# Copies and scalings recorded for ScalarE and VectorE alike, in a two-layer transformer trunk

## The chip, the core and the metric

The kernel runs on one core of a Trainium2 chip. The names of the engines are those of the profile: PE is TensorE, the matrix engine, and PEld its weight loads; DVE is VectorE and ACT is ScalarE, the two elementwise engines; POOL is GpSimd; SP issues the DMAs. The metric is device time in microseconds. Three runs of the kernel before took 2407.23, 2414.03 and 2417.83 us, so the median is 2414.03 us.

## The reference

The input is one sequence of 2048 latent tokens and 256 context tokens, 1024 wide, in float32. Two layers follow each other. In each, a conditioning vector gives shift, scale and gate; the tokens are normalized, shifted and scaled, multiplied by one input projection, mixed by two branches, multiplied by one output projection, gated and added to the stream:

```python
mod_l = jax.nn.silu(c) @ ada_w[i] + ada_b[i]
hl = rms_norm(x, norm_g[i]) * (1.0 + sc_l[:, None]) + sh_l[:, None]
# even layer: chunked gated linear attention (4 heads) || RG-LRU (512 channels), both directions
# odd layer: windowed attention (8 query heads, window 128, context keys, sink) || retention (4 heads)
y = concat([branch_a * silu(gate_a), branch_b * silu(gate_b)])
x = x + g_l[:, None] * (y @ w_out)
```

A last RMS norm gives the output. Everything is float32.

## The kernel before

**Precision and tiling.** The large products are kept near float32 by splitting each operand in two. A high part is a copy rounded to fp32r, a low part is the rest: `h = copy(raw)`, `l = raw - h`. Three products, `wh*yh`, `wl*yh` and `wh*yl`, are added in PSUM. So each weight block of 128x512 costs one copy (ACT, `wh`, L1085) and one subtraction (DVE, `wl`, L1086), 496 times in all, and so does each activation: the normalized tokens (`ya`, L1372 and L1373), the branch outputs before the output projection (L1846/L1847, L1862/L1863), the attention probabilities (`ur`, L2137/L2138). The sequence is cut into one context piece of 256 tokens and four latent pieces of 512. The projections run in `fm_block` (weights stationary, L1211) and `tm_tiles` (tokens stationary, L1189), and their results leave PSUM through copies and scalings on ACT or DVE.

**The norm.** For each 128 tokens, `scale_x` squares and sums on ACT (L1316), takes the root on POOL (L1299) and multiplies by it on DVE (`xt`, L1318). PE transposes eight 128x128 blocks (L1363) into two PSUM banks. Each block leaves PSUM with a scale and a shift per partition into a tile `tm`: in layer 0 all four of a bank on DVE (L1370), in layer 1 the second and fourth on ACT (L1368). The split follows.

**What sets the order.** The kernel is not written out instruction by instruction. All calls go to a `Recorder`, and `Plan.add` stores each with its engine, its dependencies (byte ranges of tiles) and a cost in ns. `Plan.order` then plays a list schedule: at each step it takes the engine that can start first, and on it the ready operation with the highest rank, the length of the costliest path behind it. Slots of the rings (`wr`, `wh`, `wl`, `tm`, `tmp`, PSUM banks) are given out in this play as well, where they come free. `Plan.emit` writes the calls in the order of the planned starts. Each engine works through its own queue in this order, and semaphores hold an instruction until what it reads is there. A cost marked `PORT` is for work of DVE on SBUF alone, which in the plan does not overlap with POOL's work.

Which engine a copy or a scaling has is fixed by the line that records it: `S.copy`, `S.activation` for ACT, `V.tensor_copy`, `V.tensor_scalar` for DVE. Where two engines read one PSUM bank, they wait for each other on the chip (the trace shows it below), but the plan knows only of byte ranges there, and of the order of PE's writes to one buffer.

Of the kernel before, what the change touches and what calls it, by code (L numbers as in the profile page):

```python
# [120 lines left out]
class Buffer:  # L121
    def __init__(self, ring, seq, at):
        self.ring, self.seq, self.at = ring, seq, at
        self.spans = Spans(ring.cols * 4)
        self.users = []
        self.slot = self.tile = self.last = None


class Plan:
# [5 lines left out]
    def __init__(self, nc, scratch):  # L135
        self.nc = nc
        self.ops = []
        self.tiles = {}
        self.cells = {}
        self.space = scratch.tile([128, self.WIDE], F32, name="space")  # L140
        self.space_name = self.space.tensor.name
        self.used = 0
        self.starts, self.bufs = [], []
        self.open = None


# [20 lines left out]
    def add(self, eng, fn, args, kw, after=(), line=None):  # L167
        op = len(self.ops)
        deps = {}
        out = kw["out"] if "out" in kw else (args[0] if args and isinstance(args[0], bass.AP) else None)  # L170
        outs = [x for x in (out, kw.get("accum_out")) if x is not None]
        ins = [x for x in (*args, *kw.values()) if isinstance(x, bass.AP) and not any(x is y for y in outs)]
        takes = []
        for x in ins:
            self.touch(x, op, eng, False, deps, takes)
        for x in outs:
            self.touch(x, op, eng, True, deps, takes)
        deps.pop(op, None)
        for o in after:
            if not deps.get(o):  # L180
                deps[o] = False
        self.ops.append((eng, fn, args, kw, line, deps, self.cost(eng, fn.__name__, out, ins, kw), takes))
        return op

    def touch(self, ap, op, eng, write, deps, takes):
# [28 lines left out]
        if b:  # L214
# [93 lines left out]
    def wait(self, j, e):  # L308
# [7 lines left out]
        return lat + LAT[e]  # L316

    def links(self):
        n = len(self.ops)
        succ = [[] for _ in range(n)]  # L320
        for i, o in enumerate(self.ops):
            for j, data in o[5].items():
                d = 0.0 if data is None else self.wait(j, o[0])
                if data is not None and self.ops[j][0] == o[0] and not data:
                    d = 0.0
                succ[j].append((i, d))
        return succ
# [31 lines left out]
    def order(self, key):  # L359
# [3 lines left out]
        left = [len(o[5]) for o in ops]  # L363
        at, start, landed = [0.0] * n, [0.0] * n, [0.0] * n
        self.landed = landed
# [21 lines left out]
        def wake(r):  # L387
            for k in parked[r]:
                heapq.heappush(later[ops[k][0]], (at[k], k))
            parked[r] = []  # L390
# [31 lines left out]

        def place(i, t):

            got = []
            for b in ops[i][7]:
# [3 lines left out]
                for s, us in r.free:  # L430
                    if all(done[u] for u in us) and all(s is not x[1] for x in got):
                        x = 0.0
                        for u in us:
                            d = self.wait(u, ops[i][0])
                            x = max(x, landed[u] + LAT[ops[i][0]] if d is None else start[u] + d)
                        can.append((x, len(can), s, us))
# [8 lines left out]
        for i in range(n):  # L445
            if not left[i]:
                heapq.heappush(later[ops[i][0]], (0.0, i))
        count = 0
        while count < n:
            best = None  # L450
            for e in range(5):
                if now[e]:
                    t = free[e]
# [9 lines left out]
            while later[e] and later[e][0][0] <= t:  # L463
                i = heapq.heappop(later[e])[1]
                heapq.heappush(now[e], (key[i], i))
            i = heapq.heappop(now[e])[1]
            if e == PE and last in (SMALL, QUAD) and ops[i][6][2] != last:
                same = min((x for x in now[e] if ops[x[1]][6][2] == last), default=None)
                if same:
# [3 lines left out]
                    i = same[1]  # L473
            if ops[i][6][2] == PORT and port > t:
                free[e] = t
                heapq.heappush(later[e], (port, i))
                continue
            if ops[i][7]:
                got, other = place(i, t)
                if got is None:  # L480
# [3 lines left out]
                    else:  # L484
                        parked[other].append(i)
                    continue
                for b, s, us in got:
# [3 lines left out]
                    wake(b.ring)  # L491
            occ, lat, kind = ops[i][6]
            if kind == PORT:
                port = t + occ
            elif e == PE and kind != last:
# [6 lines left out]
                elif last == TR:  # L502
                    t -= min(82.0, max(0.0, t - at[i]))
                last = kind
# [9 lines left out]
            for b in uses.get(i, ()):  # L514
                b.left -= 1
                if not b.left:
                    r = b.ring
                    hand(r.gone.pop(id(b.slot), r), b.slot, b.users)
            for k, d in succ[i]:
                at[k] = max(at[k], landed[i] + LAT[ops[k][0]] if d is None else t + d)  # L520
                left[k] -= 1
                if not left[k]:
                    heapq.heappush(later[ops[k][0]], (at[k], k))
        return start, max(free)
# [2145 lines left out]
```

## Time and profile before

| | |
|---|---|
| median of three runs | 2414.03 us |
| profiled execution, whole | 2415.39 us |
| its span, first to last instruction | 2413.6 us |
| PE busy | 2179.4 us, 90% |
| DVE busy | 1844.9 us, 76% |
| ACT busy | 1272.6 us, 53% |
| POOL busy | 277.6 us, 12% |
| mean granted clock of PE | 0.950 |

PE is the busiest engine, and it idles for 234.2 us of the span. The granted clock is a share of 2.4 GHz, and its lower level, 0.5, is 1.2 GHz. Time at the lower level counts as busy while the matrix engine does half the work. The 2415.39 us of the profiled execution are 1.4 us above the median of the runs and 1.8 us above its own span.

### The profile page before, as it was taken

To read this page: it belongs to the slowest core of one execution; us is meant where nothing else is said; L and a number is where in the kernel's file an instruction comes from. 1 tells how busy PE (TensorE), PEld (TensorE's weight loads), DVE (VectorE), ACT (ScalarE), POOL (GpSimd) and SP (SyncE) were. 2 spreads that over 40 slices of the span, in tenths; PEclk is the share of its full clock that TensorE was granted. 3 is DMA by queue.
4 is the path that set the end of the run, shared out by engine and by line. 5 is a ranking of instruction groups with operands and counts; after the bars stand their busy time and mean duration, and the time that the engine had idled before them with its cause. 6 is when DMAs were issued, how large, how long until landed. Compare 5 with 4: busy or idle time off the path is not lost. (4 is left out here: it accounts for less than half of the span.)

```text
span 2413.6 us, 43459 instructions
## 1 busy us (share of the span) xinstructions
PE 2179.4 (90%) x15721; PEld 1955.4 (81%) x15721; DVE 1844.9 (76%) x3908; ACT 1272.6 (53%) x2721; POOL 277.6 (12%) x350
## 2 busy tenths in 40 slices
PE   6999979879988989788997999979998899899998
PEld 2978768768667978687896889978898798899897
DVE  3667887897899688568776788778887768888786
ACT  2364774655566576354345444465445534566553
POOL 1000110010011000102201122001211000201021
PEclk8999989989989989798998999989999999999999
DMA  8245435544534435764444454425454233526873
GB/s 238 60 115 146 139 91 143 144 144 111 160 109 145 115 86 170 231 187 132 140 121 127 122 150 149 150 76 151 126 162 135 76 89 117 158 79 202 272 242 134
DMA packets 372616, 340.49 MB, mean 141 GB/s; under 512 B 41832, under 2 KB 318768, under 8 KB 372400
## 3 DMA queue, kind: packets, MB, share of 16 engines
q1 hardware_dynamic: 372400, 337.71, 46.8%
q8 instruction: 123, 2.02, 0.3%
q14 instruction: 93, 0.76, 0.1%
HBM read 256.31 MB, written 67.67 MB: 134 GB/s over the span
## 5 line engine op out<-in xcount | busy, mean ns | idle before, releaser
L1211 PE MATMUL psum<-wh,ya 128*128 128x256 f32 x4416 | 858.3, 290 | 13.7 <-ACT wh L1085 4.1
L1211 PEld LDWEIGHTS psum<-wh,ya 128*128 128x128 f32 x4416 | 695.4, 193 | 27.5 <-DVE ya L1373 5.1
L1189 PE MATMUL psum<-ya,wh 128*128 128x256 f32 (+2 forms) x2864 | 687.7, 325 | 23.1 <-DVE tmp L1695 9.3
L1211 PE MATMUL psum<-wl,ya 128*128 128x256 f32 x2208 | 573.6, 289 | 10.7 <-DVE wl L1086 10.7
L1189 PEld LDWEIGHTS psum<-ya,wh 128*128 128x128 f32 (+1 forms) x2864 | 484.2, 192 | 65.8 <-DVE tmp L1695 10.1
L1085 ACT CAST wh<-wr 128x512 fp32r<-128x512 f32 x496 | 303.4, 619 | 358.9 <-PE psum L1189 153.2
L1086 DVE TENSOR_TENSOR wl<-wr,wh 128x512 fp32r<-128x512 f32 x496 | 352.1, 716 | 146.9 <-ACT wh L1085 132.2
L1189 PE MATMUL psum<-ya,wl 128*128 128x256 f32 (+2 forms) x1432 | 450.5, 325 | 5.7 <-DVE wl L1086 4.3
L1211 PEld LDWEIGHTS psum<-wl,ya 128*128 128x128 f32 x2208 | 399.2, 193 | 17.2 <-DVE wl L1086 13.4
L1189 PEld LDWEIGHTS psum<-ya,wl 128*128 128x128 f32 (+1 forms) x1432 | 270.8, 192 | 27.3 <-DVE wl L1086 5.8
L2110 ACT ACTIVATE ub<-ub,s_mx 128x640 f32<-128x640 f32 (+1 forms) x128 | 104.9, 820 | 79.4 <-DVE s_mx L2101 78.4
L2137 ACT CAST ur<-psum 128x512 fp32r<-128x512 f32 (+1 forms) x184 | 93.7, 522 | 93.7 <-PE psum L2135 82.3
L2135 PE MATMUL psum<-c_k_ident,ub 128*128 128x128 f32 x624 | 126.3, 286 | 10.8 <-ACT tm L1368 5.8
L2101 DVE CUSTOM_DVE_ANT_0 ub<-psum,uc 128x640 f32<-128x640 f32 (+2 forms) x128 | 108.4, 847 | 33.5 <-PE psum L2096 30.7
L2138 DVE TENSOR_TENSOR ur<-psum,ur 128x512 fp32r<-128x512 f32 (+1 forms) x184 | 109.3, 605 | 30.7 <-ACT ur L2137 27.9
L2052 DVE TENSOR_TENSOR tmp<-tmp,ub 32x512 f32<-32x512 f32 x144 | 113.2, 786 | 12.4 <-ACT tmp L2328 6.2
L1370 DVE TENSOR_SCALAR tm<-psum,aT,shT 128x128 f32<-128x128 f32 x216 | 78.0, 407 | 38.1 <-PE psum L1363 21.0
L2135 PEld LDWEIGHTS psum<-c_k_ident,ub 128*128 128x128 f32 x624 | 79.0, 145 | 22.7 <-ACT tm L1368 9.3
L2049 POOL TENSOR_TENSOR tmp<-tmp,ub 128x512 f32<-128x512 f32 x20 | 29.7, 1483 | 389.2 <-ACT tmp L2394 217.1
L1299 POOL TENSOR_TENSOR s_rstd<-s_rstd,mhalf 128x1 f32<-128x1 f32 (+2 forms) x88 | 71.1, 810 | 6.8
L1622 ACT ACTIVATE ub<-psum,gb 128x512 f32<-128x512 f32 (+3 forms) x96 | 51.7, 584 | 32.0 <-PE psum L1621 31.7
L2114 DVE TENSOR_SCALAR ub<-ub,s_rs 128x640 f32<-128x640 f32 (+1 forms) x128 | 65.3, 549 | 1.1
(318 smaller groups left out, 3635.9 us busy)
## 6 DMA issues: line engine op xcount, KB each, us to landing
wr<-in_o_w_in_dram SPq DMA_DIRECT2D x192, 256.0 KB, 3.0
wr<-in_e_w_in_dram SPq DMA_DIRECT2D x160, 256.0 KB, 3.1
wr<-in_e_w_out_dram SPq DMA_DIRECT2D x80, 256.0 KB, 3.2
tmp<-gl SPq DMA_DIRECT2D x64, 256.0 KB, 4.1
wr<-in_o_w_out_dram SPq DMA_DIRECT2D x64, 256.0 KB, 3.4
x1l<-tmp SPq DMA_DIRECT2D x40, 256.0 KB, 3.0
xt<-x1l SPq DMA_DIRECT2D x20, 512.0 KB, 4.2
ua<-in_ada_w_dram SPq DMA_DIRECT2D x32, 256.0 KB, 4.3
```

Source lines behind the costliest of these rows:

```text
L1085: S.copy(h[:, 0:n], raw[:, 0:n])
L1086: eng.tensor_tensor(l[:, 0:n], raw[:, 0:n], h.bitcast(F32)[:, 0:n], op=ALU.subtract)
L1189: T.matmul(ps[0:m, q * w:q * w + w], lhsT=a, rhs=b, start=(q == 0 and k == 0 and i == 0), stop=(q == n // w - 1 and k == 7 and i == 2))
L1211: T.matmul(ps, lhsT=a, rhs=b, start=(ti % 2 == 0 and k == 0 and i == 0), stop=((ti % 2 == 1 or ti == len(tiles) - 1) and k == 7 and i == 2))
L1299: G.tensor_tensor(r, r, mhalf[:, 0:n], op=ALU.pow)
L1370: V.tensor_scalar(tm[:, kk], src, sc, sh, op0=ALU.mult, op1=ALU.add)
L2052: V.tensor_tensor(rot.v[to], raw.v[fr], sinb.v[fr], op=ALU.mult)
L2101: V.tensor_tensor_reduce(out=P_[:, c0:c0 + cn], in0=sc[:, so + c0:so + c0 + cn], in1=mask[:, m0:m0 + cn], scale=1.0, scalar=m, op0=ALU.add ...
L2110: tab_act(EXP, out=Ps[h], in_=Ps[h], func=AF.Exp, scale=-1.0, bias=mx[:, h:h + 1], accum_out=sm[:, h:h + 1])
L2135: T.transpose(tr[:, i * 256 + h * 128:i * 256 + h * 128 + 128], Ps[h][:, kb * 128:kb * 128 + 128], ident)
L2137: S.copy(ph[:, 0:n], tr[:, 0:n])
L2138: V.tensor_tensor(pl[:, 0:n], tr[:, 0:n], ph.bitcast(F32)[:, 0:n], op=ALU.subtract)
```

## The change

`Plan.add` asks a new function, `other_form`, whether a recorded operation can be written for the other elementwise engine as well. It can be for plain copies (`scalar.copy` and `vector.tensor_copy`), for a multiplication with an optional addition (`tensor_scalar` and `activation` with `Copy` or `Identity`), if the output has at least 64 columns, nothing is BF16 and the shapes are equal. Such an operation stands in the ready lists of both engines, with a cost for each, and in `order` the engine that takes it first keeps it. The form used is then the one emitted. Waits are worked out for the engine that did take it (`after`). The second part is in `touch`: for a PSUM buffer, an operation now also depends on the last use of the same bank by each other engine, reads included. Costs, rank rule, rings and recorded operations are the same; the ranks still go by the engine at which an operation was recorded.

```diff
+        form = self.other_form(eng, fn.__name__, args, kw)
+        if form:
+            e, fn, args, kw = form
+            self.others[op] = (e, fn, args, kw, line, deps, self.cost(e, fn.__name__, out, ins, kw), takes)
...
+    def other_form(self, eng, name, args, kw):
...
+        if name in ("copy", "tensor_copy") and not kw:
+            out, x = args
+            form = self.copies[ACT + DVE - eng], (out, x), {}
+        elif name == "tensor_scalar" and kw.get("op0") == ALU.mult and kw.get("op1", ALU.add) == ALU.add:
...
+        if n < 64 or BF16 in (out.dtype, x.dtype) or out.shape != x.shape:
+            return None
+        return (ACT + DVE - eng, *form)
...
+            if b.ring.psum:
+                hi = max(y for _, y in runs(f0, free)) - 1
+                for k in range(f0 // 512, hi // 512 + 1):
+                    used = b.banks.setdefault(k, {})
+                    for e, o in used.items():
+                        if e != eng and o != op:
+                            deps.setdefault(o, False)
+                    used[eng] = op
...
         for i in range(n):
             if not left[i]:
-                heapq.heappush(later[ops[i][0]], (0.0, i))
+                for e in at[i]:
+                    heapq.heappush(later[e], (0.0, i))
...
+            op = ops[i] if ops[i][0] == e else self.others[i]
...
-            for k, d in succ[i]:
-                at[k] = max(at[k], landed[i] + LAT[ops[k][0]] if d is None else t + d)
+            for k, data in needs[i]:
                 left[k] -= 1
-                if not left[k]:
-                    heapq.heappush(later[ops[k][0]], (at[k], k))
+                for f in at[k]:
+                    d = self.after(i, f, data)
+                    at[k][f] = max(at[k][f], landed[i] + LAT[f] if d is None else t + d)
+                    if not left[k]:
+                        heapq.heappush(later[f], (at[k][f], k))
```

65 lines are added ahead of the model code, so a line of the kernel body is 65 higher in the changed kernel (L1370 is L1435 there).

Counted in the two programs, 314 operations leave DVE for ACT and 387 leave ACT for DVE; DVE has 3983 instructions where it had 3910, and ACT 2286 where it had 2359. Matmuls, DMAs, POOL's work and the 80 table loads of ACT keep their number. The large movers are:

| line | what it is | from ACT to DVE | from DVE to ACT |
|---|---|---|---|
| L1085 | high part of a weight block, SBUF | 89 of 496 | |
| L1846 | high part of a branch output, scaled, from PSUM | 39 of 68 | |
| L2137 | high part of probabilities, from PSUM | 36 of 184 | |
| L1368 | scale and shift in the norm, from PSUM | 35 of 72 | |
| L1372 | high part of the normalized tokens, SBUF | 27 of 72 | |
| L1370 | scale and shift in the norm, from PSUM | | 113 of 216 |
| L2114 | division of the probabilities, SBUF | | 60 of 128 |
| L1318 | tokens times their root, 128x1024, SBUF | | 24 of 36 |
| others | copies and scalings on some 37 more lines | 161 | 117 |

Of the 72 groups of four scalings that empty one bank in the norm, 36 alternate between DVE and ACT before; 25 are shared by the two in the changed kernel.

**Place A**, the norm of the second latent piece in layer 0 (near 310 to 320 us in the trace of before). On DVE before, the scalings of one bank (`tm_3099`) stand among the constants of layer 1 (`smc`, `s_la`, `tmp`), the shifts (`shT`) and the LRU block (`ur`, `lru_cf`, `ub`):

```order
L1017 TENSOR_TENSOR smc_2998<-smc_2998,smc_398 128x12
L1255 TENSOR_SCALAR shT<-psum,adab 128x2
L1019 SCALAR_TENSOR_TENSOR s_la_3097<-smc_2998,smc_2994 128x12
L1370 TENSOR_SCALAR tm_3099<-psum,aT,shT 128x128 x2
L1610 TENSOR_TENSOR ur<-ub,ur 128x256
L1370 TENSOR_SCALAR tm_3099<-psum,aT,shT 128x128 x2
L1655 COPY lru_cf<-ub 128x1
L1993 TENSOR_TENSOR tmp_3109<-tmp_3109,tmp_2970 128x128
L1675 TENSOR_TENSOR ub<-ub 128x510
```

On ACT in the changed kernel, near the same place (`tm_3022` and `tm_3055` are the two tiles of the piece's first 128 tokens):

```order
L1711 ACTIVATE ub<-ub,s_119 128x510 x2
L1749 ACTIVATE tmp_3016<-psum 128x512
L1435 ACTIVATE tm_3022<-psum,shT,aT 128x128 x4
L1548 COPY ub<-uc 64x4x64 x2
L1437 CAST ya<-tm_3022 128x4x128
L1435 ACTIVATE tm_3055<-psum,shT,aT 128x128 x4
L1147 CAST wh_3066<-wr_2955 128x4x32
L1437 CAST ya<-tm_3055 128x4x128
```

All eight scalings of these tokens now stand on ACT, each bank's four in a row; before, all eight were on DVE.

**Place B**, just ahead of it: the high parts of the next weight blocks. On ACT before (`wh_3034` and `wh_3038` are read by the next matmuls of a projection):

```order
L1684 ACTIVATE tmp_3031<-psum 128x512
L1483 COPY ub<-uc 64x4x64
L1085 CAST wh_3034<-wr_2868 128x512
L1085 CAST wh_3038<-wr_2879 128x512
L1082 CAST wh_3044<-wr_2956 128x4x32 x3
L1372 CAST ya<-tm_3018 128x4x128
L1609 CAST ur<-ub 128x256
```

On DVE in the changed kernel (`wh_2973` and `wh_2978` are the high parts of the same two blocks):

```order
L1150 CAST wh_2943<-wr_2728 128x512
L1151 TENSOR_TENSOR wl_2947<-wr_2728,wh_2943 128x512
L1706 TENSOR_TENSOR ub<-ub 128x510 x2
L1150 CAST wh_2973<-wr_2856 128x512
L1150 CAST wh_2978<-wr_2873 128x512
L1311 COPY uc<-psum 128x256
L1074 TENSOR_SCALAR smc_2992<-smc_398 128x12
```

Three copies of weight blocks now stand in DVE's queue, ahead of the constants (`smc`) and of the scan behind them.

**Place C**, the subtraction that ends the split of the tokens in place A. On DVE before:

```order
L1653 SCALAR_TENSOR_TENSOR ub<-ub,lru_cf 128x510
L1015 TENSOR_TENSOR smc_2998<-smc_2998,smc_2994 128x12
L1594 SCALAR_TENSOR_TENSOR ub<-ua_137,cw,ub 128x256
L1016 TENSOR_SCALAR smc_2998<-smc_2998 128x12
L1373 TENSOR_TENSOR ya<-tm_3018,ya 128x4x128
```

On DVE in the changed kernel (`ub<-ub,s_dec` is the state recurrence of the linear attention; L1438 is L1373 before):

```order
L1600 TENSOR_TENSOR uc<-ub 64x2x64
L1082 TENSOR_TENSOR smc_2996<-smc_2996,smc_398 128x12
L1577 SCALAR_TENSOR_TENSOR ub<-ub,s_dec_3011,psum 64x128
L1084 SCALAR_TENSOR_TENSOR s_la_3118<-smc_2996,smc_2992 128x12
L1583 SCALAR_TENSOR_TENSOR ub<-ub,s_dec_3011 64x128
L1438 TENSOR_TENSOR ya<-tm_3022,ya 128x4x128
```

Between the constants' first instruction (L1009) and this subtraction DVE has 37 rows before and 48 in the changed kernel: the scalings are gone from there, and steps of the linear attention have come in front.

## Rows read from the trace of the kernel before

**Rows 1.** Head and first part of the page; the list of cores.

```profile
span 2413.6 us, 43459 instructions
PE 2179.4 (90%) x15721; PEld 1955.4 (81%) x15721; DVE 1844.9 (76%) x3908; ACT 1272.6 (53%) x2721; POOL 277.6 (12%) x350
...
core 0: 2413.6 us, clock 0.950
```

**Rows 2.** Windows of 800 us: busy us and count by engine, clock, DMA, GB/s.

```profile
0.00:800.00 800.00, 703.33 (x4826) 583.58 (x4827) 610.64 (x1355) 454.88 (x795) 69.50 (x112) 0.94 0.47 134
1600.00:2400.00 800.00, 759.48 (x5723) 712.64 (x5722) 631.67 (x1356) 419.02 (x1067) 103.59 (x116) 0.99 0.47 147
```

**Rows 3.** Windows of 10 us, the same columns.

```profile
60.00:70.00 10.00, 9.31 (x77) 8.91 (x77) 9.81 (x26) 3.00 (x6) 0.00 (x0) 1.00 0.17 54
310.00:320.00 10.00, 3.37 (x14) 2.42 (x14) 9.97 (x36) 2.97 (x9) 0.00 (x0) 0.71 0.34 111
320.00:330.00 10.00, 7.43 (x45) 6.28 (x45) 9.87 (x34) 6.94 (x22) 0.75 (x2) 0.60 0.23 62
490.00:500.00 10.00, 3.14 (x24) 2.03 (x23) 10.00 (x22) 6.43 (x12) 2.52 (x4) 0.76 0.56 170
980.00:990.00 10.00, 5.48 (x20) 4.16 (x21) 5.74 (x15) 3.64 (x12) 0.42 (x1) 0.50 1.06 367
1020.00:1030.00 10.00, 10.00 (x86) 10.00 (x86) 4.99 (x8) 2.50 (x4) 0.00 (x0) 1.00 0.68 221
2320.00:2330.00 10.00, 10.00 (x87) 10.00 (x85) 9.41 (x21) 3.95 (x9) 1.14 (x3) 1.00 0.79 240
```

**Rows 4.** Waits of PE on two-form work: us, times, longest.

```profile
PE psum L1363 <- DVE xt L1318: 22.7, 7, 5.9
PE psum L1211 <- DVE wl L1086: 10.7, 7, 7.3
...
PE psum L1620 <- DVE ur L1610: 0.2, 1, 0.2
```

**Rows 5.** Waits of PE on the rest, first and last.

```profile
PE psum L2095 <- DVE s_mx L2101: 13.8, 16, 5.0
...
PE psum L1211 <- ACT junk L1832: 0.2, 1, 0.2
```

**Rows 6.** Waits of DVE and of ACT on each other.

```profile
DVE wl L1086 <- ACT wh L1085: 132.2, 102, 6.1
ACT tm L1368 <- DVE tm L1370: 51.1, 40, 5.0
```

**Rows 7.** Groups on DVE by form: busy us, mean ns of one, idle before.

```profile
L1086 DVE TENSOR_TENSOR wl<-wr,wh 128x512 fp32r<-128x512 f32 x496 | 352.1, 716 | 146.9 <-ACT wh L1085 132.2 <-PE psum L1189 7.6 <-issue 2.0
L1370 DVE TENSOR_SCALAR tm<-psum,aT,shT 128x128 f32<-128x128 f32 x216 | 78.0, 407 | 38.1 <-PE psum L1363 21.0 <-ACT tm L1368 16.7
L2114 DVE TENSOR_SCALAR ub<-ub,s_rs 128x640 f32<-128x640 f32 x112 | 58.2, 558 | 0.9
L1318 DVE TENSOR_SCALAR xt<-xt,s_rstd 128x1024 f32<-128x1024 f32 x32 | 24.8, 774 | 8.5 <-POOL s_rstd L1299 7.4 <-ACT tm L1368 0.9
L1785 DVE COPY ua<-psum 128x512 f32<-128x512 f32 x16 | 11.0, 687 | 6.0 <-PE psum L1189 5.9
L1552 DVE COPY uc<-ub 64x128 f32<-64x128 f32 x20 | 4.4, 218 | 0.5
```

**Rows 8.** Groups on ACT by form, the same columns.

```profile
L1085 ACT CAST wh<-wr 128x512 fp32r<-128x512 f32 x496 | 303.4, 619 | 358.9 <-PE psum L1189 153.2 <-PE psum L1211 128.7 <-DMA wr<-in_e_w_in_dram 25.6
L2110 ACT ACTIVATE ub<-ub,s_mx 128x640 f32<-128x640 f32 x112 | 93.3, 833 | 70.6 <-DVE s_mx L2101 69.7
L1316 ACT ACTIVATE tm<-xt 128x1024 bf16<-128x1024 f32 x32 | 33.8, 1056 | 7.9 <-DMA xt<-in_ctx_dram 4.5 <-DVE ya L1373 1.8 <-DMA xt<-x1l 1.7
L1368 ACT ACTIVATE tm<-psum,shT,aT 128x128 f32<-128x128 f32 x72 | 31.3, 458 | 51.1 <-DVE tm L1370 51.1
L2338 ACT COPY ub<-psum 128x512 f32<-128x512 f32 x16 | 9.4, 589 | 7.4 <-PE psum L1211 7.3
```

More of the change, by code (lines that the diff above doesn't have):

```diff
@@ L144, in __init__ @@
         self.open = None
+        self.others = {}
+        self.copies = {ACT: nc.scalar.copy, DVE: nc.vector.tensor_copy}
+        self.act, self.scale = nc.scalar.activation, nc.vector.tensor_scalar
     def buffer(self, ring):
@@ L182, in add @@
         self.ops.append((eng, fn, args, kw, line, deps, self.cost(eng, fn.__name__, out, ins, kw), takes))
-        return op
+        form = self.other_form(eng, fn.__name__, args, kw)
+        if form:
+            e, fn, args, kw = form
+            self.others[op] = (e, fn, args, kw, line, deps, self.cost(e, fn.__name__, out, ins, kw), takes)
+        return op
+    def other_form(self, eng, name, args, kw):
+        if eng not in (DVE, ACT):
+            return None
[3 more added lines that the diff above has]
+        elif name == "tensor_scalar" and kw.get("op0") == ALU.mult and kw.get("op1", ALU.add) == ALU.add:
+            out, x, a, b = args
+            if b is None:
+                form = self.act, (), dict(out=out, in_=x, func=AF.Copy, scale=a)
+            elif isinstance(a, float) or isinstance(b, float):
+                return None
+            else:
+                form = self.act, (), dict(out=out, in_=x, func=AF.Identity, scale=a, bias=b)
+        elif name == "activation" and kw["func"] == AF.Identity and set(kw) == {"out", "in_", "func", "scale", "bias"}:
+            out, x = kw["out"], kw["in_"]
+            form = self.scale, (out, x, kw["scale"], kw["bias"]), dict(op0=ALU.mult, op1=ALU.add)
+        elif name == "activation" and kw["func"] == AF.Copy and set(kw) == {"out", "in_", "func", "scale"}:
+            out, x = kw["out"], kw["in_"]
+            form = self.scale, (out, x, kw["scale"], None), dict(op0=ALU.mult)
+        else:
+            return None
+        n = 1
+        for k in out.shape[1:]:
+            n *= k
+        if n < 64 or BF16 in (out.dtype, x.dtype) or out.shape != x.shape:
+            return None
+        return (ACT + DVE - eng, *form)
     def touch(self, ap, op, eng, write, deps, takes):
@@ L316, in wait, with after @@
         return lat + LAT[e]
+    def after(self, j, e, data):
+        if data is None:
+            return 0.0
+        return 0.0 if self.ops[j][0] == e and not data else self.wait(j, e)
     def links(self):
@@ L322, in links @@
             for j, data in o[5].items():
[L323 to L326, printed above, removed]
+                succ[j].append((i, self.after(j, o[0], data)))
         return succ
@@ L363, in order @@
         left = [len(o[5]) for o in ops]
-        at, start, landed = [0.0] * n, [0.0] * n, [0.0] * n
+        start, landed = [0.0] * n, [0.0] * n
+        at = [{o[0]: 0.0} for o in ops]
+        for i, o in self.others.items():
+            at[i][o[0]] = 0.0
+        needs = [[] for _ in range(n)]
+        for i, o in enumerate(ops):
+            for j, data in o[5].items():
+                needs[j].append((i, data))
         self.landed = landed
@@ L387, in wake @@
         def wake(r):
-            for k in parked[r]:
-                heapq.heappush(later[ops[k][0]], (at[k], k))
+            for k, e in parked[r]:
+                heapq.heappush(later[e], (at[k][e], k))
             parked[r] = []
@@ L451, in order @@
             for e in range(5):
+                for q in (now[e], later[e]):
+                    while q and done[q[0][1]]:
+                        heapq.heappop(q)
                 if now[e]:
@@ L464, in order @@
                 i = heapq.heappop(later[e])[1]
-                heapq.heappush(now[e], (key[i], i))
+                if not done[i]:
+                    heapq.heappush(now[e], (key[i], i))
             i = heapq.heappop(now[e])[1]
@@ L478, in order @@
             if ops[i][7]:
-                got, other = place(i, t)
+                got, other = place(i, e, t)
                 if got is None:
```

17 lines of the change are left out of this document (9 added, 8 removed).

## The prediction

> **What bounds the kernel now.** I read the head of the page first: PE is busy for 2179.4 of 2413.6 us, so it idles for 234.2 us, and its mean clock is 0.950 [rows 1]. The idle time has to be found before any edit can be priced. The windows of 800 us say where it is not: from 1600 us on PE is busy for 759.5 of 800 us at a clock of 0.99, while in the first third it has 703.3 at 0.94 [rows 2]. What can be won lies before 1600 us.
>
> Windows of 10 us say what the other engines did meanwhile [rows 3]. From 310 to 330 us PE was busy for 3.37 and 7.43 us and DVE for 9.97 and 9.87, with ACT at 2.97 and 6.94. From 490 to 500 DVE had 10.00, ACT 6.43, PE 3.14. Of the 240 such windows up to 2400 us, 62 show DVE at 9.3 or more (the first at 60 us, the last at 2320). They hold 78 us of PE's idle time, and 48 of them, with ACT under 7.5, hold 64 us. So about a quarter of the idle time falls where DVE's queue is full and ACT has room. The rest lies where neither is full (980 us: DVE 5.74, ACT 3.64, PE 5.48): chains of dependent steps and loads.
>
> Then the waits of PE by releaser. I put them into two heaps. In the first, the releaser is an operation that the change can move or the subtraction right behind one: 33 rows with 104 waits, 118.0 us together, from the tokens' scaling L1318 with 22.7 us down to 0.2 us [rows 4]. In the second it is something else (scores, state steps, DMAs): 22 rows, 77 waits, 98.5 us, from 13.8 us down [rows 5]. The two make 216.5 of the 234.2 us.
>
> Idle time costs twice. At 980 us the clock stood at 0.50, the 1.2 GHz level, and 20 matmuls ran in 10 us; at 1020 us, at the 2.4 GHz level, 86 did [rows 3]. A mean clock of 0.950 is 0.05 x 2413.6 = 121 us of full-clock work not done [rows 1], against 234 us of idle time: 0.52 us for each us of idle. I price idle time that goes or comes at 1.52.
>
> **The work that moves.** Leaving DVE are 314 operations. L1370: 113 x 407 ns = 46.0 us on DVE, and at the 458 ns of the same step on ACT 51.8 us there. L1318: 24 x 774 ns = 18.6 us; on ACT the square of the same tile takes 1056 ns without a pointer operand, and a pointer adds about 105 ns (833 ns for 640 columns with one, against 619 + 128 x 0.85 = 728 without, the 0.85 ns a column from 619 and 1056), so 24 x 1161 = 27.9 us. L2114: 60 at about 550 = 33 us on DVE, 60 at about 825 = 49 us on ACT. The other 117 lie between 218 ns (64x128) and 687 ns each: 26 to 80 us, taken as 44 by their shapes, and 47 on ACT. Sum: 142 us off DVE, 176 us onto ACT [rows 7, 8].
>
> Leaving ACT are 387. The largest, 89 copies of a 128x512 block from SBUF (619 ns on ACT, 55.1 us), have no like on DVE in the trace. The bounds are 218 ns (a copy a quarter as long) and 716 ns (two sources, same size). The single-source scalings cost 558 ns for 640 columns and 774 for 1024, that is 0.5625 ns a column; 218 + 384 x 0.5625 = 434 ns is what I take, since those rows also read SBUF alone: 38.6 us, with 19.4 and 63.7 us as the ends. The Trainium skill, "VectorE: DVE Perf Modes", section "The perf-mode tier table", gives float32 copies between SBUF tiles twice the rate of operations with two tensors; an estimate from its cycles, (150 + 256) / 0.96 = 423 ns, would make the 89 copies 37.6 us. No run here shows it yet for a target in fp32r. By the same slope L1372 costs 27 x 434 = 11.7 us. From PSUM DVE needs 687 ns for 512 columns where ACT needs 589: L2137 23, L1846 19, L1368 14 us. The other 161 lie between 35 and 111 us, taken as 74. Sum: 181 us onto DVE, 206 us off ACT [rows 7, 8].
>
> So DVE gains about 40 us net (1845 to 1885 us, 78%) and ACT loses about 30 (1273 to 1243). This is no relief of the fuller engine. What can help is when the moves happen: copies go to DVE where the plan finds it free, and leave it where it is full.
>
> **What it ends.** Place A is the best case in sight: eight scalings, 8 x 407 ns = 3.3 us, leave DVE where PE idled for 6.63 + 2.57 = 9.2 us in 20 us [rows 3, 7]. That is 36% of the idle time there. I take a third for the first heap as a whole: 39 of 118 us, with nothing and all 118 as the ends. From the second heap I take nothing: its releasers have one form. Two kinds of waits between the elementwise engines shrink as well: 132.2 us of DVE waiting for the high part of a weight block, and 51.1 us of ACT waiting for DVE on the same `tm` bank [rows 6]. In the norm 36 banks were shared by two engines and 25 will be. PE was waiting for few of these, so they are part of the third.
>
> **What it adds.** 40 us more in DVE's queue. In most windows DVE has room (5.74 and 4.99 of 10 at 980 and 1020 us [rows 3]) and PE never sees it; that cover is gone where DVE is full. Place C shows it: the subtraction behind the eight scalings has 48 rows of DVE's queue since the constants ahead of it instead of 37, and matmuls wait for it. I take 17 us of new waits, a little under half of 40, with 0 and 40 as the ends. ACT, 53% busy, takes its slower forms without a price, except in the rivals. The bank dependencies add no work: the 51.1 us show that the engines already waited there.
>
> Sum: 39 - 17 = 22 us less idle, x 1.52 = 33 us. The profiled execution's 2415.4 us become 2382; its time stands 1.4 us above the median of the runs, so 2381 us. Ends alone would give 0 - 40 = +61 us and 118 - 0 = -179 us; I hold neither likely, since nearly every place mixes both.
>
> **The rivals.**
> *More of the first heap goes.* Half of it, 59 us, with no new waits: 59 x 1.52 = 90 us, 2325 us. For it speak the 64 us in windows with DVE full and ACT free; against it that DVE ends up with more work, and that the same scans and state steps keep its queue full there.
> *No change.* The waits change names: DVE's queue ends at the same moment in each full stretch because the one-form work sets it, and PE idles as before, 2414 us. The matmuls around place A stand in nearly the same order, and the 98.5 us of the second heap stay.
> *Slower through DVE's queue.* A copy taken by DVE because it is free stands ahead of a subtraction or a state step which becomes ready a moment later. If none of the first heap goes and half of the 40 us is felt by PE, 20 x 1.52 = 31 us: 2445 us. It decides from the point where more new wait arises than the third that goes, 39 us. Places B and C speak for it, ACT's and DVE's shorter waits for each other against it.
> *Slower through ACT's longer forms.* The moved scalings take 176 instead of 142 us, 386 ns more for each L1318, which PE awaits most [rows 4]. If that is felt in full and nothing goes, 34 x 1.52 = 52 us; felt by half, 26 us: 2440 us. The Trainium skill, "ScalarE: Activation LUTs", section "Rules for kernel authors", says to use VectorE, not ScalarE, for plain multiplications and additions. By that rule the change errs in these 314. The trace agrees on each instruction (407 against 458 ns [rows 7, 8]) but shows ACT idle 47% of the time, so I give it little.
>
> **How the numbers follow.** Forecast 47%, own range 2355 to 2402; more goes 14%; no change 17%; slower through DVE's queue 14%; through ACT 8%. A difference under about 0.5%, 12 us, can't be told from none here. Faster is the forecast and the first rival, 61%; same 17%; slower 22%. The range has to take in the no-change case and reach towards both outer ones: 2322 to 2435 leaves out some of the larger gain and the greater part of the slower cases, about 2 in 10.
>
> **What the changed profile would show.** If I am right: PE idle near 212 us and a clock above 0.95; DVE about 78% busy, ACT about 52%; the rows of PE's waits on L1318, L1605, L1609 and the weight copies down by a third; fewer 10 us windows with DVE full and PE under 8 between 300 and 900 us; DVE's copies of weight blocks near 434 ns. I am wrong if DVE's weight copies take about 700 ns, if PE's waits on state steps and subtractions grow by more than 39 us, or if PE's idle time falls by more than 50 us.

## The result, and the profile after

The changed kernel takes 2384.36 us (median of 4 runs, 2383.96 to 2384.65); the kernel before took 2415.93 us beside it (4 runs). The ratio is 0.9872, 95% interval 0.9841 to 0.9903: 1.3% faster. The profiled execution took 2383.96 us. Lines of the kernel's body are 65 higher than before (L1086 is L1151, L1318 is L1383).

The head of the page, its first part, and the list of cores:

```profile
span 2382.2 us, 43338 instructions
...
PE 2155.3 (90%) x15721; PEld 1944.9 (82%) x15721; DVE 1878.7 (79%) x3981; ACT 1250.3 (52%) x2648; POOL 277.9 (12%) x350
```
```profile
core 0: 2382.2 us, clock 0.951
```

Against [rows 1] the span is 31.4 us shorter, and this is not mainly idle time: PE idles for 2382.2 - 2155.3 = 226.9 us, 7.3 us less than before. PE's *busy* time fell by 24.1 us, with the same 15721 matmuls. DVE has 34 us more work and ACT 22 us less.

Windows (busy us and count by engine, clock, DMA share, GB/s), answering [rows 2] and [rows 3]:

```profile
0.00:800.00 800.00, 705.22 (x4892) 587.78 (x4893) 614.25 (x1350) 462.47 (x821) 71.00 (x114) 0.93 0.47 135
270.00:280.00 10.00, 1.76 (x8) 1.76 (x9) 9.96 (x17) 7.85 (x12) 1.39 (x1) 0.50 0.16 60
320.00:330.00 10.00, 3.62 (x31) 2.41 (x29) 9.84 (x39) 5.87 (x20) 0.00 (x0) 0.83 0.33 110
330.00:340.00 10.00, 5.76 (x25) 5.46 (x26) 8.46 (x27) 7.08 (x29) 1.36 (x2) 0.50 0.33 90
```

In 800 us PE is 66 matmuls further on than before (4892 against 4826). The two windows from 320 us are place A, the norm of the second latent piece. Its scalings are on ACT now, yet DVE is as full as before (9.84) and PE idles for 6.38 + 4.24 = 10.6 of 20 us, where it was 9.2 [rows 3]. The relief that I read off this place did not come.

PE's waits (engine, line, releaser: us, times, longest):

```profile
PE psum L1428 <- ACT xt L1383: 20.9, 6, 6.0
PE psum L1276 <- DVE wl L1151: 16.5, 9, 5.3
PE psum L1276 <- DVE tmp L1750: 13.6, 4, 11.2
PE psum L2160 <- DVE s_mx L2166: 13.3, 19, 3.6
...
PE psum L1428 <- DVE xt L1383: 3.8, 1, 3.8
...
PE psum L1684 <- ACT ur L1674: 0.6, 1, 0.6
```

Split as before, the first heap (two-form work and the subtraction behind it) went from 118 to about 95 us [rows 4], the second from 98.5 to about 118 us [rows 5]. The wait for the tokens' scaling moved from DVE to ACT and did not shrink (22.7 to 20.9 + 3.8). L1619's waits for L1605 and L1609, 9.8 + 6.0 us before, are down to 0.6 (L1684 for L1674). Nearly new are the waits for L1750, a gating step that only DVE can do: 0.7 us before, and now a single one of 11.2 us among others. PE stands from 267.0 to 278.2 us for it. The timeline of DVE shows the second part of that stretch (start, us, engine, line):

```profile
269.90 0.69 DVE L1715 SCALAR_TENSOR_TENSOR ub<-ub 128x510 f32<-128x510 f32 x1 [0.89 <-ACT ub L1711]
270.51 1.21 DVE L1730 TENSOR_TENSOR_SCAN tmp<-ub,zero 128x510 f32<-128x510 f32 x1
271.64 1.19 DVE L1723 TENSOR_TENSOR_SCAN ub<-ub 128x510 f32<-128x510 f32 x1
...
274.19 0.42 DVE L1670 CAST ur<-tmp 128x512 fp32r<-128x512 f32 x1
274.53 0.48 DVE L1659 SCALAR_TENSOR_TENSOR ub<-ua,cw,ub 128x256 f32<-128x256 f32 x1
274.92 2.29 DVE L1718 TENSOR_TENSOR_SCAN ub<-ub,lru_cf 128x510 f32<-128x510 f32 x1
277.13 0.45 DVE L1659 SCALAR_TENSOR_TENSOR ub<-ua,cw,ub 128x256 f32<-128x256 f32 x1
277.51 0.68 DVE L1750 SCALAR_TENSOR_TENSOR tmp<-tmp,psum 128x512 f32<-128x512 f32 x1
```

Scans and convolution steps stand ahead of L1750 without a gap, and between them the cast L1670, which was ACT's and takes 0.42 us. No other operation in the stretch shown came from ACT. What fills the queue was DVE's before, and nearly all of it has one form.

DVE's and ACT's waits for each other, answering [rows 6], in two views:

```profile
DVE wl L1151 <- ACT wh L1150: 112.0, 78, 4.7
DVE tm L1435 <- ACT tm L1435: 13.4, 17, 4.6
```
```profile
ACT tm L1435 <- DVE tm L1435: 11.0, 18, 1.9
```

Groups by form on DVE and on ACT (busy us, mean ns, idle before), answering [rows 7] and [rows 8]:

```profile
L1151 DVE TENSOR_TENSOR wl<-wr,wh 128x512 fp32r<-128x512 f32 x496 | 346.3, 703 | 130.2 <-ACT wh L1150 112.0 <-PE psum L1308 4.4 <-PE psum L1254 3.5
L1435 DVE TENSOR_SCALAR tm<-psum,aT,shT 128x128 f32<-128x128 f32 x103 | 39.0, 405 | 39.2 <-PE psum L1428 25.2 <-ACT tm L1435 13.4
L1150 DVE CAST wh<-wr 128x512 fp32r<-128x512 f32 x89 | 38.1, 431 | 27.8 <-PE psum L1276 12.7 <-PE psum L1254 7.0 <-DMA wr<-in_o_w_in_dram 3.8
```
```profile
L1435 ACT ACTIVATE tm<-psum,shT,aT 128x128 f32<-128x128 f32 x113 | 48.8, 458 | 35.9 <-PE psum L1428 23.7 <-DVE tm L1435 11.0 <-DVE ya L1438 0.8
L2179 ACT ACTIVATE ub<-ub,s_rs 128x640 f32<-128x640 f32 x53 | 43.6, 828 | 29.0 <-DVE s_rs L2177 28.3 <-DVE s_s L2625 0.5
L1383 ACT ACTIVATE xt<-xt,s_rstd 128x1024 f32<-128x1024 f32 x23 | 26.4, 1147 | 5.6 <-POOL s_rstd L1364 5.5
```

All prices of single operations came as bounded. What they add up to at PE needed experiments.

### The profile page after: what moved, and what is told of

Its sections match the earlier page's. It is cut to its first block, busy times and chain, and to the rows that moved or that the text cites. A ratio compares the mean times of both kernels' runs of the same rounds, so it can differ in the third digit from the quotient of the medians.

```text
span 2382.2 us, 43338 instructions
## 1 busy us (share of the span) xinstructions
PE 2155.3 (90%) x15721; PEld 1944.9 (82%) x15721; DVE 1878.7 (79%) x3981; ACT 1250.3 (52%) x2648; POOL 277.9 (12%) x350
## 5 line engine op out<-in xcount | busy, mean ns | idle before, releaser
L1276 PE MATMUL psum<-wh,ya 128*128 128x256 f32 x4416 | 863.9, 290 | 34.5 <-DVE tmp L1750 13.6
L1276 PEld LDWEIGHTS psum<-wh,ya 128*128 128x128 f32 x4416 | 698.2, 193 | 51.3 <-DVE tmp L1750 14.8
L1254 PE MATMUL psum<-ya,wh 128*128 128x256 f32 (+2 forms) x2864 | 679.2, 322 | 20.6 <-DVE tmp L1760 12.2
L1276 PE MATMUL psum<-wl,ya 128*128 128x256 f32 x2208 | 571.8, 289 | 16.5 <-DVE wl L1151 16.5
L1254 PEld LDWEIGHTS psum<-ya,wh 128*128 128x128 f32 (+1 forms) x2864 | 475.2, 189 | 64.9 <-DVE tmp L1760 13.3
L1151 DVE TENSOR_TENSOR wl<-wr,wh 128x512 fp32r<-128x512 f32 x496 | 346.3, 703 | 130.2 <-ACT wh L1150 112.0
L1254 PE MATMUL psum<-ya,wl 128*128 128x256 f32 (+3 forms) x1432 | 439.4, 321 | 0.3 <-DVE wl L1151 0.3
L1150 ACT CAST wh<-wr 128x512 fp32r<-128x512 f32 x407 | 250.1, 618 | 340.9 <-PE psum L1276 157.7
L1276 PEld LDWEIGHTS psum<-wl,ya 128*128 128x128 f32 x2208 | 400.4, 194 | 21.5 <-DVE wl L1151 18.8
L1254 PEld LDWEIGHTS psum<-ya,wl 128*128 128x128 f32 (+1 forms) x1432 | 265.0, 189 | 19.8 <-issue 2.0
L2202 ACT CAST ur<-psum 128x512 fp32r<-128x512 f32 (+1 forms) x148 | 74.7, 513 | 106.6 <-PE psum L2200 98.7
L1364 POOL TENSOR_TENSOR s_rstd<-s_rstd,mhalf 128x1 f32<-128x1 f32 (+2 forms) x88 | 77.1, 880 | 6.4
L2114 POOL TENSOR_TENSOR tmp<-tmp,ub 128x512 f32<-128x512 f32 x20 | 28.3, 1416 | 394.9 <-DVE tmp L2459 229.3
L1435 DVE TENSOR_SCALAR tm<-psum,aT,shT 128x128 f32<-128x128 f32 x103 | 39.0, 405 | 39.2 <-PE psum L1428 25.2
L1428 PE MATMUL psum<-c_k_ident,xt 128*128 128x128 f32 x256 | 43.5, 303 | 27.2 <-ACT xt L1383 20.9
```

The costliest lines, as they stand in the source:

```text
L1150: S.copy(h[:, 0:n], raw[:, 0:n])
L1151: eng.tensor_tensor(l[:, 0:n], raw[:, 0:n], h.bitcast(F32)[:, 0:n], op=ALU.subtract)
L1254: T.matmul(ps[0:m, q * w:q * w + w], lhsT=a, rhs=b, start=(q == 0 and k == 0 and i == 0), stop=(q == n // w - 1 and k == 7 and i == 2))
L1276: T.matmul(ps, lhsT=a, rhs=b, start=(ti % 2 == 0 and k == 0 and i == 0), stop=((ti % 2 == 1 or ti == len(tiles) - 1) and k == 7 and i == 2))
L1364: G.tensor_tensor(r, r, mhalf[:, 0:n], op=ALU.pow)
L2202: S.copy(ph[:, 0:n], tr[:, 0:n])
```

## The experiments

The change has two parts: the *choice* (second forms, and a planner that gives each to the engine that is free first) and the *orders* (the plan learns that two engines on one PSUM bank go one after the other; `touch` keeps them by the engine at which an operation was recorded, not by the one that takes it). The forecast gave the whole gain to the choice and nothing to the orders. Theory 1 is the forecast's; theory 2 puts the gain into the orders; theory 3 says that any change of the plan's input re-makes a greedy order, and the gain is one lucky throw, one of many orders that the plan could as well have ended up with. Theories 4 to 6 came with the results.

For each kernel I split the span in three. *Idle* is span minus PE's busy time. *Work* is busy time at full clock: over all windows of 10 us, PE's busy us times the granted clock, summed. *Slow* is the rest, busy time lost to the lower clock. "Banks" counts the norm's banks, of 72, that ACT and DVE share in the order; "tm" sums the waits of either of the two for the other at those steps, in us. Median is the time over the runs; the other columns are of one profiled execution.

```
kernel                      median   span  = idle  + work   + slow  banks  tm
before                      2415.9  2413.6  234.2   2099.7   79.7    36    68
before, second throw        2415.5  2414.3  230.1   2094.9   89.2    36    69
orders alone                2399.4  2402.7  223.1   2087.9   91.8    36    37
orders alone, second        2397.2  2395.5  222.0   2081.9   91.6    36    37
choice alone                2433.1  2431.3  257.7   2093.9   79.7    59    80
choice alone, second        2438.6  2437.1  258.0   2100.0   79.2    59    82
both (the changed kernel)   2384.4  2382.2  226.9   2081.3   74.0    25    24
both, second throw          2376.4  2376.1  220.5   2083.3   72.2    25    25
orders, choice to ACT only  2386.2  2384.1  220.7   2086.2   77.2    43    29
orders, choice to DVE only  2420.1  2415.9  242.4   2083.4   90.0     4    12
choice alone, SBUF only     2419.3  2419.9  246.5   2094.3   79.0    36    53
orders, choice SBUF only    2391.4  2384.3  222.9   2083.1   78.2    36    29
before, no shared bank      2403.3  2402.5  224.2   2095.6   82.6     0     0
both, no shared bank        2385.8  2381.8  219.7   2079.9   82.1     0     0
```

The split is not sharper than some 10 us: between the two throws of the kernel before, which take the same time, work differs by 4.8 us and slow by 9.5.

**The two parts apart.** Orders alone: no operation gets a second form.

```diff
     def other_form(self, eng, name, args, kw):
-        if eng not in (DVE, ACT):
-            return None
+        return None
```

> The orders between the two elementwise engines on one PSUM bank are recorded, but no operation has a second form. Theory 1 (the gain is the choice by the free engine): the gain is gone, 2414 us within 8, as before. Theory 2 (the gain is that the plan now knows of the waits inside a bank): 2385 us within 8, as after. Theory 3 (the gain is one throw of a greedy plan, which any change of its input re-makes): anything from 2375 to 2435 us, and nothing in the trace that belongs to banks.

2399.38 us, ratio 0.9929 (0.9907 to 0.9951). Half of the gain, without moving a single operation. Theory 1 (2414 within 8) and theory 2 (2385 within 8) both miss; the time lies between them.

Choice alone: the block that records the orders is taken out.

```diff
-            if b.ring.psum:
-                hi = max(y for _, y in runs(f0, free)) - 1
...
-                    used[eng] = op
```

> Second forms as in the changed kernel, without the orders on one bank. Theory 1: 2384 us within 8, as after; ACT's and DVE's waits for each other inside a tm bank come back to about 50 us, but PE does not see them. Theory 2: 2414 us within 8. Theory 3: anything from 2365 to 2430 us.

2433.05 us, ratio 1.0063 (1.0042 to 1.0083): slower than before. Theory 1 expected 2384 and falls; theory 2 expected 2414 and falls as well. Singly the parts give -16 and +17.5 us, which would add up to nothing; together they give -31.6.

DVE's and ACT's waits inside the norm's banks, from the trace of choice alone (L1425 and L1427 are L1368 and L1370 before):

```profile
DVE tm L1425 <- ACT tm L1427: 32.1, 22, 4.4
DVE tm L1427 <- ACT tm L1427: 14.6, 17, 4.7
...
DVE tm L1427 <- ACT tm L1425: 3.2, 6, 0.6
DVE tm L1425 <- ACT tm L1425: 2.8, 5, 0.6
```
```profile
ACT tm L1427 <- DVE tm L1427: 11.8, 21, 2.1
ACT tm L1425 <- DVE tm L1427: 7.8, 11, 1.9
```

Free to choose and blind to the bank, the plan splits 59 of 72 banks (all 36 of layer 1 and 23 of layer 0), as if both engines then worked side by side. The program makes them take turns, and DVE, the fuller engine, stands 53 us at them, with its whole queue behind it (17 us before, 13 after). Summed from the 7000th matmul on, PE's waits are 100 us, against 76 before and 77 after; up to there they are 142, 141 and 136. So the loss lies in the second part of the span.

**A second throw of each.** All four kernels again, with nothing changed but a latency allowance of the plan:

```diff
-SLACK, SLACK_DMA = 150.0, 1000.0
+SLACK, SLACK_DMA = 149.0, 1000.0
```

> The kernel before, with the plan's slack on every latency 149 instead of 150 ns: nothing of what the plan may do changes, only the order that it ends up with. It says how far one throw of the plan lies from the next. Theory 3 (the gain is a throw): 10 us or more from 2415, to either side. Theory 4 (choice and bank orders each have their own effect, the choice helps only with the orders): within 6 us of 2415.

> The changed kernel with 149 instead of 150 ns. Theory 4: within 6 us of 2384. Theory 3: 10 us or more away, as likely above as below, and perhaps no better than before.

> Bank orders alone, with 149 instead of 150 ns. Theory 4 (orders alone give about 16 us): within 6 us of 2399. Theory 3: 10 us or more away.

> Choice alone, with 149 instead of 150 ns. Theory 4 (choice without the orders loses some 17 us, since DVE stands for about 50 us in tm banks that ACT still reads): within 6 us of 2433, and again some 50 us of DVE waiting for ACT on tm. Theory 3: 10 us or more away, more likely nearer to 2415.

Before: 2415.52 us, ratio 0.9999 (0.9988 to 1.0009). Both: 2376.36, 0.9837 (0.9818 to 0.9856). Orders alone: 2397.20, 0.9925 (0.9908 to 0.9943). Choice alone: 2438.64, 1.0093 (1.0073 to 1.0113). In the kernel before some 700 of PE's matmuls then stand at another place of its program or use another slot, with both parts some 6300, with one part 1500 to 1600. The time moves by 0.4, 8, 2 and 6 us. Theory 3 falls: throws differ by less than the parts do, and the four kernels keep their ranks. It is one second throw of each, and the one of the kernel before changed the order least; below, a difference of up to 8 us between kernels of one throw each counts as not told apart. Theory 4 holds: the choice pays only with the orders. Its 6 us for both was too narrow; that throw gained 8.

**Which direction.** Only DVE's operations get a second form, then only ACT's:

```diff
-        if eng not in (DVE, ACT):
+        if eng != DVE:
             return None
```
```diff
-        if eng not in (DVE, ACT):
+        if eng != ACT:
             return None
```

> Only operations recorded for DVE have a second form, so work can leave DVE for ACT and none goes the other way; bank orders as after. Theory 1 (relief of DVE where it is full): DVE's busy time falls from 1845 to about 1700 us, windows of 10 us with DVE at 9.3 or more fall from 62 to under 50, the time is 2385 us or a little less (2370 to 2395). Rival (ACT's longer forms on the path, 386 ns more for a tokens' scaling): 2415 to 2440 us. Theory 3: between 2370 and 2435 us without a relation to DVE's full windows.

> Only operations recorded for ACT have a second form, so work can leave ACT for DVE, none the other way; bank orders as after. Theory 1: DVE's busy time rises to about 2000 us (84%), its queue is full more often (over 75 windows of 10 us), and the time is 2414 us or more (2410 to 2440). Rival (what helps is the shorter copy, 431 ns against 619, and the shorter wait of the subtraction for it): 2385 us or less. Theory 3: between 2370 and 2435 us without a relation to DVE's load.

To ACT only: 2386.20 us, 0.9870 (0.9852 to 0.9889). To DVE only: 2420.10 us, 1.0013 (0.9999 to 1.0027). The busy times, first to ACT only, then to DVE only:

```profile
PE 2163.4 (91%) x15721; PEld 1947.9 (82%) x15721; DVE 1738.1 (73%) x3615; ACT 1408.5 (59%) x3014; POOL 275.8 (12%) x350
```
```profile
PE 2173.5 (90%) x15721; PEld 1957.1 (81%) x15721; DVE 1999.7 (83%) x4295; ACT 1105.4 (46%) x2334; POOL 281.2 (12%) x350
```

PE's wait for the tokens' scaling in the two:

```profile
PE psum L1428 <- ACT xt L1383: 22.3, 6, 6.5
```
```profile
PE psum L1428 <- DVE xt L1383: 39.1, 11, 6.5
```

With the orders in place the choice acts as theory 1 had it: relief of DVE (51 windows of 10 us with DVE at 9.3 or more, one over what was expected, 62 before) is worth 11 to 13 us against orders alone, a fuller DVE (98 windows) costs 21 to 23, and here the scaling waits in DVE's queue (39.1 us, 27.5 with orders alone). ACT's longer forms, 1147 against 774 ns, cost PE nothing that shows. Choosing both ways, 2384 and 2376 us in two throws, is not told apart from choosing to ACT alone.

**Which operations.** Second forms only where the source lies in SBUF, once without and once with the orders:

```diff
+        b = self.buffer_of(x)
+        if b and b.ring.psum:
+            return None
         return (ACT + DVE - eng, *form)
```

> Choice without bank orders, but only for operations that read SBUF; those that read PSUM keep their engine, so 36 banks of the norm are shared as before, not 59. Theory 4 (choice alone loses because it splits PSUM banks over two engines that then wait for each other): the loss of 17 to 23 us is gone, 2395 to 2417 us. Rival (choice alone loses because a free engine takes a copy ahead of work that PE awaits): 2425 to 2440 us.

> The changed kernel with bank orders, second forms only for operations that read SBUF. Theory 5 (the copies and scalings in SBUF bring what goes beyond the orders): 2380 to 2390 us. Rival (it is the steps that read PSUM, the norm's above all, which the orders let the plan keep in one bank on one engine): 2396 to 2402 us, as with orders alone.

Without orders: 2419.31 us, 1.0021 (1.0007 to 1.0035). With: 2391.43 us, 0.9904 (0.9879 to 0.9928). So 11 to 17 of the 17 to 23 us that choice alone loses are the steps that read PSUM; about 6 us of loss stay, and the first is 2 us beyond what theory 4 allowed. With the orders, 2391 us misses theory 5 (2380 to 2390) and its rival (2396 to 2402) alike: the SBUF moves bring 6 to 8 us beyond orders alone, no more than throws differ by, and the PSUM steps turn from a loss into a gain of 7 us, 15 against the second throw.

**Is a shared bank dear in itself?** First the kernel before with its own planner, where ACT takes every second bank of the norm whole; then both parts, with a rule that pins a bank to the engine of its first step:

```diff
-                    if kk in KA[i]:
+                    if KA[i] and kh % 2:
```
```diff
             start[i], done[i] = t, True
+            if i in self.bank_of:
+                for j in self.in_bank[self.bank_of[i]]:
+                    if not done[j]:
+                        pinned.add((j, ACT + DVE - e))
...
-                if not done[i]:
+                if not done[i] and (i, e) not in pinned:
```

> The kernel before, plan and costs untouched; only the norm of the latent pieces gives ACT every second bank whole (four steps) instead of two steps in each bank. No bank of the norm is shared, 36 before. Theory 6 (the waits inside shared banks, 99 us of ACT and DVE, end at PE): 2395 to 2405 us. Rival (PE doesn't feel them; the orders help because the plan stops laying other work as if they weren't there): 2410 to 2420 us.

> The changed kernel with one rule more: the first step of a PSUM bank to be given out pins the bank's other two-form steps to the same engine, so none of the norm's 72 banks is shared (25 after the change, 36 before). Theory 6 (waits inside shared banks end at PE): a little faster than the changed kernel's 2384 us, 2368 to 2382. Rival (with the orders the plan already lays the shared banks where nobody waits; to share one is then a gain, since two engines empty it sooner): 2384 to 2400 us.

The first took 2403.32 us, 0.9950 (0.9933 to 0.9967); the second 2385.79 us, 0.9876 (0.9857 to 0.9895). One line in the kernel before, with as many steps on each engine as ahead of it, takes 10 to 12 us off, as theory 6 expected. It is a single throw, but the gain lies where the waits lay: all 68 us of them stand between 1000 and 1900 us, in the norm of layer 1. Up to 960 us PE does 5992 matmuls before and 5987 with this line; from there to 1900 us (columns as in [rows 2]), first before, then with the line:

```profile
960.00:1900.00 940.00, 847.62 (x5941) 775.20 (x5940) 705.10 (x1437) 450.37 (x1025) 132.12 (x146) 0.95 0.47 142
```
```profile
960.00:1900.00 940.00, 854.53 (x6034) 783.31 (x6033) 717.66 (x1458) 453.57 (x1040) 137.91 (x147) 0.95 0.47 144
```

So these waits did end at PE, as far as one throw can show.

The pin adds nothing to the changed kernel: theory 6 expected 2368 to 2382 us and misses, its rival 2384 and more. The rival's reason, that the plan lays the shared banks well because it knows of them, does not fit the programs. Of the 25 shared banks of the changed kernel 24 are in layer 0. There all four steps of a bank are recorded for DVE, so `touch` records no order between them, and the plan does not see that one of them on ACT has to wait. In layer 1, where the orders exist, one bank of 36 is shared. The 24 us of waits that are left (L1435 for L1435) stand before 700 us, all in layer 0. Taking them away gave nothing that can be told from a throw, so a wait in a shared bank does not always reach PE; why those of layer 1 did and these did not stays open.

No version tried beats the changed kernel by more than a throw.

**Where the orders act.** They also hold PE, which writes a bank while ACT or DVE reads another part of it. Two groups of matmuls, by form, before, with orders alone, with choice alone, and after (line, shape, count, busy us, mean ns, idle before):

```profile
L1842 PE MATMUL psum<-c_k_ident,so 128*128 128x128 f32 x136 | 33.6, 305 | 17.6 <-DVE so L1835 11.9 <-ACT ya L1846 3.7 <-DVE ya L1847 1.7
L1506 PE MATMUL psum<-ua,uc 64*128 64x128 f32 x288 | 30.4, 305 | 7.9 <-ACT uc L1491 6.4
```
```profile
L1906 PE MATMUL psum<-c_k_ident,so 128*128 128x128 f32 x136 | 34.9, 296 | 13.4 <-DVE so L1899 13.3
L1570 PE MATMUL psum<-ua,uc 64*128 64x128 f32 x288 | 24.2, 300 | 6.0 <-ACT uc L1555 6.0
```
```profile
L1899 PE MATMUL psum<-c_k_ident,so 128*128 128x128 f32 x136 | 34.7, 303 | 17.9 <-DVE so L1892 12.4 <-ACT ya L1903 4.9 <-DVE ya L1903 0.3
L1563 PE MATMUL psum<-ua,uc 64*128 64x128 f32 x288 | 30.1, 299 | 4.6 <-ACT uc L1548 1.5 <-DVE ub L1565 1.3 <-DVE uc L1548 0.9
```
```profile
L1907 PE MATMUL psum<-c_k_ident,so 128*128 128x128 f32 x136 | 34.6, 299 | 12.3 <-DVE so L1900 12.3
L1571 PE MATMUL psum<-ua,uc 64*128 64x128 f32 x288 | 24.0, 299 | 3.5 <-ACT uc L1556 3.2 <-DVE uc L1556 0.3
```

The transposes of L1842 waited for the readers of their own bank (3.7 and 1.7 us); with the orders, with or without the choice, those waits are gone. The 288 small matmuls of L1506 take 30 us without and 24 us with the orders, though each lasts the same 300 ns: they start closer to each other. One group of 16 from PE's timeline, before and after (start, us):

```profile
188.13 1.79 PE L1506 MATMUL psum<-ua,uc 64*128 64x128 f32 x16
```
```profile
187.86 1.16 PE L1571 MATMUL psum<-ua,uc 64*128 64x128 f32 x16
```

These matmuls have 64 rows. In the trace they start in pairs, 6 to 7 ns apart, mostly one pair every 105 ns. In the group of before the last pairs have come apart: single matmuls start 111 ns behind each other, and one starts 416 ns behind the one ahead, held by a semaphore. Of the 288, 112 start within 10 ns of the one ahead before, and 136 after. So this busy time is partly waiting and partly pairs that no longer start together. The timeline of PE after the change shows why a wait can hide there:

```profile
259.16 0.40 PE L1684 MATMUL psum<-ur 128*128 128x510 f32 x1
259.39 0.40 PE L1685 MATMUL psum<-ur 128*128 128x510 f32 x1
259.63 0.39 PE L1686 MATMUL psum<-ur 128*128 128x510 f32 x1
```

Matmuls start 0.23 us apart and are shown 0.40 us long, so a pause of up to 0.17 us between two of them leaves no gap, and a longer one is shown shorter than it is. PE has 206 to 220 gaps in the kernels with the orders and 244 to 264 in those without. In the table the sum under "work" is 2080 to 2088 us in all eight kernels with the orders and 2094 to 2100 in all six without them: with the same matmuls, some 13 us of busy time go, 6 of them in L1506, and no view calls them idle. Whether the orders between ACT and DVE bring the gain or those that hold PE, no run separates.

## Why the prediction came out

The time was forecast as 2381 us and is 2384; of its reasons some hold and one fails. That the sum came so close is luck. The forecast had 22 us less idle time and 11 us less loss to the clock; measured were 7.3 and 5.7. The difference was made up by 18.4 us of work that stands closer, for which it had no term.

**The prices held.** DVE's copy of a weight block takes 431 ns where 434 was taken. (The Trainium skill, "VectorE: DVE Perf Modes", section "The perf-mode tier table", gives float32 copies between SBUF tiles twice the rate of operations with two tensors, and the estimate from that page's cycles was 423 ns; the trace agrees within 2%, also for a target in fp32r.) L1383 takes 1147 ns on ACT (1161 taken), L2179 828 (about 825). DVE gained 34 us (40), ACT lost 22 (30).

**The two terms of the waits were of the right kind, and off in size.** "A third of the first heap goes", 39 us: 23 went. "17 us of new waits": about 19 came, 11.2 of them in one place, the wait for L1750. L1211's waits for this step (L1276 for L1750 after) sum to 13.5 to 13.7 us in both throws of the changed kernel and of choice alone, 9.0 with the choice to ACT only, and 1.4 with orders alone, so they come with the choice. But the rival in which a copy taken by DVE stands ahead of dependent work explains little of it: one moved step of 0.42 us stands there, and with the choice to ACT only DVE takes nothing from ACT. DVE's own steps stand in another order; what put them there the runs do not show. Net, the named waits fell by 3 us and PE's idle time by 7, not 22. At place A, the best case in sight, nothing was won: what filled DVE there has one form.

**The step that failed is the one on the bank orders**: that they "add no work", because the 51.1 us of [rows 6] showed that the engines already waited there. They did wait; the plan before did not know it and laid other work as if they didn't. Telling it is worth 16 to 18 us by itself, and without it the choice is a loss of 17 to 23 us, most of it from the steps that read PSUM, where it splits 59 of the norm's banks. The forecast credited the choice with what belongs to the pair. The Trainium skill, "PSUM — Partial Sum Buffer", section "Terms", says that two engines on one bank and quadrant at once are an error, and that the compiler keeps them apart. The trace agrees in that the engines take turns within a bank (68 us of such waits in the norm before). The plan needs that rule as much as the program does.

**The price of 1.52 per idle us is no constant.** It was too high from the start: the 121 us behind it apply the mean clock to the whole span, while PE's busy time weighed by its clock, window by window, gives 79.7 us lost before, 0.34 for each idle us. Kernels with 219 to 225 us of idle time have spans from 2376 to 2403 us. Of the 31.4 us gained, 7.3 are idle time, 18.4 work that stands closer, and 5.7 less lost to the lower clock. From orders alone to both, idle time does not fall (223.1 and 226.9 us); most of the gain is in "slow", 91.8 to 74.0, and 91.6 to 72.2 in the second throws. Why the same idle time costs less clock there I did not settle: of stretches below 0.95, in windows of 10 us, there are 26 with orders alone and 21 with both, but 25 with the choice to ACT only, where "slow" is as low as 77.2.

**The signs that I had named.** DVE 79% and ACT 52%: right. Clock above 0.95: 0.951, barely. PE idle near 212 us: wrong, 226.9. Waits on L1605 and L1609 down: 15.8 to 0.6 us, more than forecast; on L1318 down: no; on the weight blocks: PE's waits for `wh` and `wl` went from 23.9 to 17.9 us, a quarter. Windows with DVE full and PE under 8 between 300 and 900 us: 10 to 8, while over the whole span the windows with DVE full rose from 62 to 71. None of the three signs of being wrong showed: DVE's weight copies take 431 ns, PE's idle time fell by 7 us, and the waits of the second heap, state steps among them, grew by 19.5. Of the rivals, "no change" was right on idle time, and wrong on the time, since it looked at idle time alone.

## What to carry to other kernels

Give a scheduler the rules by which the hardware and the program make engines take turns before giving it freedom of choice; a choice made blind to them can cost more than it brings. When two edits come together, price them as a pair: here neither sign nor size of the one could be read without the other. And where matmuls overlap in the profile, look at how far apart they start, not only at idle time.

## What the runs showed that was not expected

Some 13 us of PE's busy time went with the same matmuls: short pauses under the shown tail of a matmul (0.40 us long, 0.23 us apart), tails ahead of gaps, and pairs of small matmuls that had come apart. A change of 1 ns in the plan's allowance re-makes hundreds to thousands of lines of the order and moved the time by 8 us at most. And 17 us of DVE's and 51 us of ACT's waiting inside shared banks, which looked harmless beside a PE busy for 90% of the span, belonged to banks whose sharing cost 10 to 12 us, as a one-line edit of the kernel before showed, while 24 us of the same kind in layer 0 of the changed kernel cost nothing that shows.
